# GDN decays without a DRAM round trip, another address for the weight buffers, one modulation sum per chunk in the first MLP, and SSD decay rows issued one step later

## The chip, the cores and the metric

The program runs on one core of a Trainium2 chip, alone. The metric is the time of one execution on the device in microseconds (us). The kernel before was run three times: 2693.74, 2696.27 and 2699.25 us.

## The reference

The input is 512 tokens of width 1024 (`x`), and eight stages follow each other, all in float32: a gated-delta-rule mixer (GDN), a convolutional feed-forward (ffn0), a chunked attention, a second feed-forward (ffn1), an S5 state-space mixer, an MLP (mlp0), an SSD mixer, an MLP (mlp1), and a final norm. The pieces that the change touches:

```python
# GDN, per head and chunk of 64 tokens
gcum  = cumsum(g)                                  # g: log decay per token
decay = where(causal, exp(gcum[:, None] - gcum[None, :]), 0)
m     = where(strict, (k*beta) @ k.T * decay, 0)   # then (m + I)^-1 applied to v*beta, k*beta*exp(gcum)
attn  = (q @ k.T) * decay
q_dec = q * exp(gcum)
...
# second block: modulation from a condition vector c
mod = silu(c) @ ada_w[i] + ada_b[i]                # 1024 x 6144 per layer
sh1, sc1, g1, sh2, sc2, g2 = split(mod, 6)
h = rmsnorm(x) * (1 + sc) + sh
mlp: a = relu(h @ w1); y = (a*a) @ w2
...
# SSD, per head and chunk of 128 tokens
l_mat  = exp(segsum(dt*a))                         # decays inside a chunk
y_diag = (C B^T * l_mat) @ xdt
y_off  = (C @ state_before) * exp(cumsum(dt*a))
```

## The kernel before, in words

**Layout.** Activations lie with the feature on the partition and the 512 tokens along the row: eight tiles `h` of 128x512. To keep float32 accuracy TensorE (PE) gets every operand as a sum of two reduced floats, `hi` and `lo`. So one chunk of weights (128x1024, 512 KB, one column block of 128 outputs) costs a DMA into `raw` (L296), a cast to `hi` on ScalarE (ACT, L306), a subtraction to `lo` on VectorE (DVE, L307), and 24 matmuls of 128x128 by 128x512 in `mm_ch`: for each of 8 row blocks `hi` by `xh` (L348), `hi` by `xl` (L349), `lo` by `xh` (L350). `raw`, `hi` and `lo` have three buffers each; `next()` keeps the split one chunk ahead and the loads three. The moving operand is named by the stage: `xh`/`xl` for a stage's normed input, `ah`/`al` for the inner activations of feed-forward and MLP, `goh`, `aoh`, `soh` for the outputs of GDN, attention and S5 or SSD.

**Where tiles lie.** Tiles get their addresses in the order in which the program makes them. `xh` and `xl` come before `rb` and `rcol` (L248), and all weight buffers and the pools of the stages come behind them. Each 128-wide block of weights and each moving tile row begins at a multiple of 512 bytes from its buffer's start, so the distance between a weight block and a moving tile, taken modulo 512 bytes, is fixed per pair of buffers.

**Order.** Instructions run in order on each engine's queue, and so do the DMA issues on SyncE's (SP). A scheduler at build time sets the order in each queue from the order in the code and the buffers that come free.

**GDN.** `gdn_gates` makes the cumulated log decays of all heads, writes them as rows to DRAM (`grow`), and then, for each of 8 heads, loads them back to all partitions (`gd`), subtracts the column's value and adds a mask (on GpSimd, POOL, L683 and L684, or, for the first four heads, on DVE, L687), takes the exponential on ACT (L689) and writes the 128x512 result to DRAM (`gD`). `gdn_core` of a head loads `gD` back as `D`, loads `exp` rows as `eg`, multiplies `q` into `eg` on POOL (L840), makes `ke` (ACT, L821), the products `s<-kq` (PE, L834), `N` and `AT` (DVE, L836 and L838), and inverts: 15 small steps `td`, `Xd` on DVE (L850, L852) on the diagonal blocks, which come back through DRAM (`Nd<-gN`), a mask product `Nm` on POOL (L873), and block steps on PE. `gdn_proj` makes q, k and v of a head: projection, convolution, Silu (L778).

**Background work.** `next()` calls `step_bg(self.bgrate)`: that many steps of a queue of generators per chunk of weights. `ada_bg(q)` makes a third of the modulation vector: 32 steps, each a 512 KB load (`araw<-ada`, two buffers) and one multiply-add into `acc` (DVE, L1145), then 16 small matmuls `bg<-par,acc` (L1150) that sum it. `shift_bg` makes a product of the modulation shift with weight columns: multiply-adds into `sacc` (L1402), and a matmul `bg<-ones,sacc` (L1393) per chunk. In ffn1 the rate is 1 or 2, and its last value, 2, stays on in mlp0, where the queue holds `shift_bg` for SSD, `ada_bg(2)` and `shift_bg` for mlp1.

**SSD.** Four groups of 8 heads. The decays' rows lie in DRAM (`srow`). Per group two `D` tiles (128x2048, four heads each) and four `E` tiles are loaded from it, the `E` with two rows spread over 64 partitions each. `ssd_exps` subtracts on DVE, and step 1 of `ssd_core` takes the exponential.

Of the kernel before, what the change touches and what calls it, by code (L numbers as in the profile page):

```python
# [224 lines left out]
class Net:  # L225
    def __init__(self, ctx, tc, aps, pcols, out):
# [21 lines left out]
        rc = self.cpool.tile([P, 8], F32, name="rcol")  # L248
# [384 lines left out]
    def gdn_gates(self, gg, g1, wk):  # L633
# [31 lines left out]
        ga = gg.tile([P, 3, 32], F32, name="gga")  # L665
# [12 lines left out]
        self.gD = self.dram.tile([8, P, T], F32, name="gD")  # L678
        for hd in range(8):
            d = wk.tile([P, 4, P], F32, tag="Nm", name=self.nm("gd"))  # L680
            nc.sync.dma_start(out=d, in_=self.grow[0, 4 * hd:4 * hd + 4, :].partition_broadcast(P))
            if hd > 3:
                gp.tensor_tensor(out=d, in0=d, in1=bc(ga[:, 0, 4 * hd:4 * hd + 4], P), op=ALU.subtract)  # L683
                gp.tensor_tensor(out=d, in0=d, in1=self.p("nincl").unsqueeze(1).to_broadcast([P, 4, P]), op=ALU.add)  # L684
            else:
                for c in range(4):
                    v.scalar_tensor_tensor(out=d[:, c, :], in0=d[:, c, :], scalar=ga[:, 0, 4 * hd + c:4 * hd + c + 1],  # L687
                                           in1=self.p("nincl"), op0=ALU.subtract, op1=ALU.add)
            s.activation(d, d, AF.Exp)  # L689
            nc.sync.dma_start(out=self.gD[hd], in_=d.rearrange("p c t -> p (c t)"))  # L690

    def gdn(self):
# [3 lines left out]
        with es:  # L696
# [4 lines left out]
            self.eye16 = g1.tile([32, 256], F32, name="geye")  # L701
# [16 lines left out]
            nc.sync.dma_start(out=self.eye16, in_=self.aps["eye16"])  # L718
# [6 lines left out]
            for name, i in self.gdn_seq():  # L725
# [41 lines left out]
    def gdn_proj(self, wk, hd):  # L767
        s = self.nc.scalar
        taps = [self.p(f"a_conv{j}") for j in range(4)]
        kq = wk.tile([P, 2, T], F32, tag="kq", name=self.nm("kq"))  # L770
# [8 lines left out]
        return kq, vv  # L779

    def gdn_core(self, wk, hd, kq, vv):
# [19 lines left out]
        Dt, eg = tl("D"), tl("eg")  # L801
        nc.sync.dma_start(out=Dt.rearrange("p c t -> p (c t)"), in_=self.gD[hd])
# [1269 lines left out]
```

## Time and profile before

| what | value |
|---|---|
| median of three runs | 2696.27 us |
| the profiled execution: its own time | 2695.84 us |
| the profiled execution: its span in the trace | 2694.0 us |
| PE busy, DVE busy, ACT busy, POOL busy | 2614.5, 1943.8, 1182.6, 114.8 us |
| granted PE clock, mean over the span | 0.989 |

The span is what the trace covers from the first to the last instruction; 1.84 us of the execution's time lie around it. The stages stand in the span, roughly: GDN to 380 us, ffn0 to 760, attention to 1020, ffn1 to 1380, S5 to 1580, mlp0 to 1960, SSD to 2325, mlp1 to the end. A granted clock of 1.00 is PE's higher level, 2.4 GHz, and 0.5 the lower, 1.2 GHz. The time printed for one matmul is its latency; how fast a row of them goes is read from the distance of their starts.

### The profile page before, as it was taken

The page shows a single profiled execution, that of the slowest core. Times are in us where ns is not written, and L with a number is a line of the kernel's source. Part 1 is how long each engine was busy: PE and PEld are TensorE (multiplying, and loading weights), DVE is VectorE, ACT ScalarE, POOL GpSimd, SP SyncE. Part 2 cuts the span into 40 slices and gives each one's busy share as a digit, 9 for nine tenths or more (in the row PEclk, how much of TensorE's full clock was granted, in tenths as well). Part 3 has the DMA queues.
Part 4 walks back from the last instruction along what each step waited for, and adds up shares of the span by engine and source line. Part 5 has one row for each costly group of instructions (what it writes and reads, how often), then busy time and mean ns, then how long its engine had stood idle before and what let it go on. Part 6 is the DMA issues. An engine that isn't in the chain of part 4 may idle for free. (4 is left out here: it accounts for less than half of the span.)

```text
span 2694.0 us, 36720 instructions
## 1 busy us (share of the span) xinstructions
PE 2614.5 (97%) x13978; PEld 2108.1 (78%) x13978; DVE 1943.8 (72%) x3614; ACT 1182.6 (44%) x1868; POOL 114.8 (4%) x150
## 2 busy tenths in 40 slices
PE   8899999999999999999998999899998999999998
PEld 6777777888877877888877788788877877788886
DVE  7887889997656588979888577644588778844443
ACT  7555554343445465423264352233464434533332
POOL 0211100000002110000002000000000000000000
PEclk9999999999999999999999999899999999999999
DMA  5433223544334337766639348433233432232322
GB/s 163 139 84 86 68 87 91 170 150 143 107 115 111 99 89 234 237 200 219 215 100 298 118 136 277 160 99 94 86 118 110 141 104 98 85 102 94 99 97 71
DMA packets 172705, 356.33 MB, mean 132 GB/s; under 512 B 44048, under 2 KB 81648, under 8 KB 171504
## 3 DMA queue, kind: packets, MB, share of 16 engines
q1 hardware_dynamic: 163056, 349.78, 41.2%
q10 hardware_dynamic: 9472, 4.20, 0.5%
q8 instruction: 110, 1.80, 0.3%
q14 instruction: 67, 0.55, 0.1%
HBM read 324.00 MB, written 25.72 MB: 130 GB/s over the span
## 5 line engine op out<-in xcount | busy, mean ns | idle before, releaser
L306 ACT CAST hi<-raw 128x1024 fp32r<-128x1024 f32 (+1 forms) x416 | 433.0, 1042 | 868.7 <-PE mm L349 718.8
L348 PE MATMUL mm<-xh,hi 128*128 128x512 f32 x1824 | 734.4, 403 | 17.9 <-ACT hi L306 9.2
L350 PE MATMUL mm<-xh,lo 128*128 128x512 f32 x1824 | 723.7, 398 | 2.1 <-DVE lo L307 2.0
L349 PE MATMUL mm<-xl,hi 128*128 128x512 f32 x1824 | 722.0, 396 | 0.0
L307 DVE TENSOR_TENSOR lo<-raw,hi 128x1024 fp32r<-128x1024 f32 (+1 forms) x416 | 503.5, 1211 | 214.0 <-ACT hi L306 208.9
L348 PEld LDWEIGHTS mm<-xh,hi 128*128 128x128 f32 x1824 | 346.6, 190 | 95.7 <-ACT hi L306 11.2
L350 PEld LDWEIGHTS mm<-xh,lo 128*128 128x128 f32 x1824 | 345.9, 190 | 81.3 <-DVE lo L307 3.9
L349 PEld LDWEIGHTS mm<-xl,hi 128*128 128x128 f32 x1824 | 346.5, 190 | 73.8 <-issue 2.3
L348 PE MATMUL mm<-ah,hi 128*128 128x512 f32 x864 | 337.5, 391 | 0.0
L349 PE MATMUL mm<-al,hi 128*128 128x512 f32 x864 | 336.4, 389 | 0.0
L350 PE MATMUL mm<-ah,lo 128*128 128x512 f32 x864 | 336.3, 389 | 0.0
L581 DVE SCALAR_TENSOR_TENSOR h<-mm,mods,h 128x512 f32<-128x512 f32 x96 | 71.8, 749 | 177.1 <-PE mm L350 176.8
L348 PEld LDWEIGHTS mm<-ah,hi 128*128 128x128 f32 x864 | 162.2, 188 | 34.5 <-ACT hi L306 1.2
L609 DVE SCALAR_TENSOR_TENSOR cv<-cvr,par,cv 128x511 f32<-128x511 f32 (+2 forms) x248 | 187.0, 754 | 2.7 <-ACT cv L607 0.8
L350 PEld LDWEIGHTS mm<-ah,lo 128*128 128x128 f32 x864 | 162.2, 188 | 34.0 <-DVE lo L307 0.3
L349 PEld LDWEIGHTS mm<-al,hi 128*128 128x128 f32 x864 | 162.2, 188 | 33.6
L1145 DVE SCALAR_TENSOR_TENSOR acc<-araw,condt,acc 128x1024 f32<-128x1024 f32 x93 | 119.1, 1280 | 34.6 <-DMA araw<-ada 34.0
L579 DVE TENSOR_TENSOR h<-mm,h 128x512 f32<-128x512 f32 x112 | 76.6, 686 | 51.5 <-PE mm L350 51.1
L350 PE MATMUL mm<-soh,lo 128*128 128x512 f32 x256 | 100.5, 393 | 0.5 <-DVE lo L307 0.5
L348 PE MATMUL mm<-soh,hi 128*128 128x512 f32 x256 | 100.8, 400 | 0.1
L349 PE MATMUL mm<-sol,hi 128*128 128x512 f32 x256 | 100.7, 394 | 0.0
L600 DVE TENSOR_TENSOR cvr<-mm,rb 128x512 f32<-128x512 f32 x112 | 76.6, 684 | 32.6 <-PE mm L350 25.1
(526 smaller groups left out, 3602.0 us busy)
## 6 DMA issues: line engine op xcount, KB each, us to landing
raw<-mlp SPq DMA_DIRECT2D x128, 512.0 KB, 3.5
araw<-ada SPq DMA_DIRECT2D x96, 512.0 KB, 4.4
raw<-f_up SPq DMA_DIRECT2D x88, 512.0 KB, 3.8
raw<-m_in SPq DMA_DIRECT2D x40, 512.0 KB, 4.5
raw<-a_in SPq DMA_DIRECT2D x32, 512.0 KB, 4.3
raw<-f_down SPq DMA_DIRECT2D x32, 512.0 KB, 4.5
raw<-b_kv SPq DMA_DIRECT2D x16, 512.0 KB, 3.6
raw<-s_glu SPq DMA_DIRECT2D x16, 512.0 KB, 4.2
```

The source lines that it names most:

```text
L306: self.nc.scalar.copy(hi[:, :sz], raw[:, :sz])
L307: self.nc.vector.tensor_tensor(out=lo[:, :sz], in0=raw[:, :sz], in1=hi[:, :sz].bitcast(F32), op=ALU.subtract)
L348: self.nc.tensor.matmul(ps, a, xh, start=(start and k == 0), stop=False)
L349: self.nc.tensor.matmul(ps, a, xl, start=False, stop=False)
L350: self.nc.tensor.matmul(ps, b, xh, start=False, stop=(stop and k == n - 1))
L579: nc.vector.tensor_tensor(out=self.h[ot], in0=ps, in1=self.h[ot], op=ALU.add)
L581: nc.vector.scalar_tensor_tensor(out=self.h[ot], in0=ps, scalar=g[:, ot:ot + 1], in1=self.h[ot], op0=ALU.mult, op1=ALU.add)
L600: nc.vector.tensor_tensor(out=pr, in0=ps, in1=r, op=ALU.mult)
L609: nc.vector.scalar_tensor_tensor(out=t[:, d:], in0=ps[:, :T - d], scalar=taps[n - 1 - d], in1=t[:, d:], op0=ALU.mult, op1=ALU.add)
L1145: v.scalar_tensor_tensor(out=acc, in0=raw, scalar=cond[:, k:k + 1], in1=acc, op0=ALU.mult, op1=ALU.add)
```

## The change

- **GDN.** The loop over heads leaves `gdn_gates`. A new `gdn_decay`, called at the start of a head's `gdn_proj`, loads `D` and `eg` of that head from `grow` and makes `D` in its place: two 128x512 operations on DVE and the exponential on ACT. `gD` and its 16 transfers are gone. `eg` and `Nm` go from POOL to DVE. `Xd` is loaded from DRAM by a DMA per head instead of being copied from `geye`.
- **Addresses.** `rcol` grows from 8 to 24 floats, so all that is made behind it lies 64 bytes further; `geye` goes and `gga` is padded.
- **PSUM banks.** Before the last output projection of GDN, and in the last quarter of attention's, `set_lanes()` opens all five `mm` banks instead of two.
- **Background.** `ada_bg` waits one step more before its matmuls; `shift_bg` issues its matmul one step later, with three `sacc` buffers; `mlp` sets `bgrate = 1`.
- **SSD.** The code issues the fourth `E` tile and both `D` tiles of the next group one step later; the second half's subtraction moves into the next group's step 0.

The core of the diff:

```diff
-        rc = self.cpool.tile([P, 8], F32, name="rcol")
+        rc = self.cpool.tile([P, 24], F32, name="rcol")
...
-        self.gD = self.dram.tile([8, P, T], F32, name="gD")
-        for hd in range(8):
-            d = wk.tile([P, 4, P], F32, tag="Nm", name=self.nm("gd"))
-            nc.sync.dma_start(out=d, in_=self.grow[0, 4 * hd:4 * hd + 4, :].partition_broadcast(P))
-            if hd > 3:
-                gp.tensor_tensor(out=d, in0=d, in1=bc(ga[:, 0, 4 * hd:4 * hd + 4], P), op=ALU.subtract)
-                gp.tensor_tensor(out=d, in0=d, in1=self.p("nincl").unsqueeze(1).to_broadcast([P, 4, P]), op=ALU.add)
-            else:
-                for c in range(4):
-                    v.scalar_tensor_tensor(out=d[:, c, :], in0=d[:, c, :], scalar=ga[:, 0, 4 * hd + c:4 * hd + c + 1],
-                                           in1=self.p("nincl"), op0=ALU.subtract, op1=ALU.add)
-            s.activation(d, d, AF.Exp)
-            nc.sync.dma_start(out=self.gD[hd], in_=d.rearrange("p c t -> p (c t)"))
+
+    def gdn_decay(self, wk, hd):
...
+        rows = slice(4 * hd, 4 * hd + 4)
+        d, eg = [wk.tile([P, 4, P], F32, tag=t, name=self.nm(t), bufs=2) for t in ("D", "eg")]
+        for x, out in enumerate((d, eg)):
+            nc.sync.dma_start(out=out, in_=self.grow[x, rows, :].partition_broadcast(P))
+        nc.vector.tensor_tensor(out=d, in0=d, in1=bc(self.ga[:, 0, rows], P), op=ALU.subtract)
+        nc.vector.tensor_tensor(out=d, in0=d, in1=self.p("nincl").unsqueeze(1).to_broadcast([P, 4, P]), op=ALU.add)
+        nc.scalar.activation(d, d, AF.Exp)
+        return d, eg
...
+                    if i == 2:
+                        self.set_lanes()
                     self.proj_out("a_out", [outs.pop(2 * i), outs.pop(2 * i + 1)], 512, 2, last=(i == 3))
...
-        Dt, eg = tl("D"), tl("eg")
-        nc.sync.dma_start(out=Dt.rearrange("p c t -> p (c t)"), in_=self.gD[hd])
-        nc.sync.dma_start(out=eg, in_=self.grow[1, 4 * hd:4 * hd + 4, :].partition_broadcast(P))
...
-        gp.tensor_tensor(out=eg, in0=r3(q, 4), in1=eg, op=ALU.mult)
+        v.tensor_tensor(out=eg, in0=r3(q, 4), in1=eg, op=ALU.mult)
...
-        v.tensor_copy(Xd.rearrange("p j i -> p (j i)"), self.eye16)
+        nc.sync.dma_start(out=Xd.rearrange("p j i -> p (j i)"), in_=self.aps["eye16"])
...
-        gp.tensor_tensor(out=m, in0=N, in1=self.lv.unsqueeze(1).to_broadcast([P, 4, P]), op=ALU.mult)
+        v.tensor_tensor(out=m, in0=N, in1=self.lv.unsqueeze(1).to_broadcast([P, 4, P]), op=ALU.mult)
...
             yield
         yield
+        yield
         ps = self.bank("bg")
...
-            if i > 1:
+            if i > 2:
                 ps = self.bank("bg")
-                nc.tensor.matmul(ps[:, 0:1], accs[i - 2], self.ones[:, 0:1], start=True, stop=True)
-                v.tensor_copy(out[:, i - 2:i - 1], ps[:, 0:1])
+                nc.tensor.matmul(ps[:, 0:1], accs[i - 3], self.ones[:, 0:1], start=True, stop=True)
+                v.tensor_copy(out[:, i - 3:i - 2], ps[:, 0:1])
...
             acts = {}
+            self.bgrate = 1
...
+            if g:
+                self.ssd_exps(g, 1)
...
-            for j in range(4):
-                E = self.stile("E")
-                nc.sync.dma_start(out=E, in_=AP(self.srow.tensor, self.srow.offset + (32 + 8 * g + 2 * j) * T,
-                                                [[T, 2], [0, 64], [1, T]]))
-                S["E"].append(E)
+            for j in range(3):
+                self.ssd_erow(g, j)
...
+            if j == 1:
+                self.ssd_erow(g, 3)
+            if j == 2 and g < 3:
+                self.ssd_rows(g + 1, 0)
...
-            if j % 2 == 1 and g < 3:
-                self.ssd_rows(g + 1, j // 2)
...
-            self.ssd_exps(g + 1, 1)
+            self.ssd_rows(g + 1, 1)
```

What this does to the order on the engines stands here for three places. The first is ACT's queue in GDN, at the second head's `ke` (L821 before, L818 after; `junk` are the row sums of squares that precede it, `gd` the exponentials of the decays). Before:

```order
85 L814 ACTIVATE junk_1000,ss_978<-s_146_979 128x128
86 L689 ACT_TABLE_LOAD
87 L689 ACTIVATE gd_326<-gd_326 128x512
88 L689 ACTIVATE gd_332<-gd_332 128x512
89 L814 ACTIVATE junk_1002,ss_978<-s_148_981 128x128
90 L821 ACTIVATE ke_1011<-s_146_979,gge 128x128
```

The same place in the changed kernel:

```order
84 L811 ACTIVATE junk_949,ss_925<-s_140_928 128x128
85 L811 ACTIVATE junk_951,ss_925<-s_140_928 128x128
86 L811 ACTIVATE junk_953,ss_925<-s_140_928 128x128
87 L811 ACTIVATE junk_955,ss_925<-s_140_928 128x128
88 L818 ACTIVATE ke_958<-s_138_926,gge 128x128 x4
```

The exponentials of other heads' decays no longer stand between the row sums and `ke`. They stand further up and further down the queue, one table load each: three heads' before this place, the fourth during the first head's inversion.

The second is DVE's queue in the middle of mlp0, at the last multiply-adds of `ada_bg(2)`. `lo` is the split of a weight chunk, `ra` and `al` the activations of an up-projection chunk, and `mods` takes up what the `bg<-par,acc` matmuls on PE have summed. Before:

```order
2604 L307 TENSOR_TENSOR lo_16123<-raw_16038,hi_16122 128x1024
2605 L1145 SCALAR_TENSOR_TENSOR acc_15471<-araw_16043,condt,acc_15471 128x1024
2606 L1612 TENSOR_TENSOR ra_16071<-mm_16046,ra_16071 128x512
2607 L1145 SCALAR_TENSOR_TENSOR acc_15471<-araw_16084,condt,acc_15471 128x1024
2608 L568 TENSOR_TENSOR al_16075<-ra_16071,ah_16074 128x512
2609 L307 TENSOR_TENSOR lo_16176<-raw_16082,hi_16175 128x1024
2610 L1145 SCALAR_TENSOR_TENSOR acc_15471<-araw_16087,condt,acc_15471 128x1024
2611 L1612 TENSOR_TENSOR ra_16115<-mm_16090,ra_16115 128x512
2612 L1153 TENSOR_TENSOR mods<-bg_16128,par 128x32
```

The changed kernel, at the last multiply-add:

```order
2624 L1144 SCALAR_TENSOR_TENSOR acc_15582<-araw_16682,condt,acc_15582 128x1024
2625 L307 TENSOR_TENSOR lo_16069<-raw_15990,hi_16068 128x1024
2626 L1613 TENSOR_TENSOR ra_16020<-mm_15995,ra_16020 128x512
2627 L1144 SCALAR_TENSOR_TENSOR acc_15582<-araw_16723,condt,acc_15582 128x1024
2628 L568 TENSOR_TENSOR al_16024<-ra_16020,ah_16023 128x512
2629 L1144 SCALAR_TENSOR_TENSOR acc_15582<-araw_16764,condt,acc_15582 128x1024
2630 L307 TENSOR_TENSOR lo_16110<-raw_16031,hi_16109 128x1024
2631 L1613 TENSOR_TENSOR ra_16061<-mm_16036,ra_16061 128x512
```

The multiply-adds keep their pace of two per weight chunk; the scheduler has drawn them up as before. `mods` followed one row behind the last of them, and now comes 55 rows and 21 weight chunks (`lo`) later, and with it the matmuls on PE: they stood in the middle of the chunk that PE had just begun, and now stand 20 chunks behind the one that the last multiply-add was drawn up with.

The third is SP's queue in SSD, at the transfers of the first group's last and the second group's first `E`. Before:

```order
685 L296 DMA raw_18377<-m_in 128x1024
686 L1784 DMA D_18368<-srow 128x2048
687 L1873 DMA E_18216<-srow 128x1x512
688 L1873 DMA E_18824<-srow 128x1x512
689 L296 DMA raw_18437<-m_in 128x1024
690 L1873 DMA E_18826<-srow 128x1x512
691 L1784 DMA D_18490<-srow 128x2048
692 L296 DMA raw_18515<-m_in 128x1024
```

The changed kernel:

```order
676 L296 DMA raw_18340<-m_in 128x1024
677 L1785 DMA D_18374<-srow 128x2048
678 L1790 DMA E_18312<-srow 128x1x512
679 L1790 DMA E_18789<-srow 128x1x512
680 L296 DMA raw_18402<-m_in 128x1024
681 L1790 DMA E_18791<-srow 128x1x512
682 L1785 DMA D_18512<-srow 128x2048
683 L296 DMA raw_18478<-m_in 128x1024
```

Nothing moved: the transfers of `D`, `E` and the weights follow each other as before, here and in all four groups.

## Rows read from the trace of the kernel before

**Rows 1.** The page: busy us by engine.
```profile
PE 2614.5 (97%) x13978; PEld 2108.1 (78%) x13978; DVE 1943.8 (72%) x3614; ACT 1182.6 (44%) x1868; POOL 114.8 (4%) x150
```

**Rows 2.** GDN by windows; PEclk is the granted clock, then DMA share, GB/s.
```profile
core 0: us, PE busy (x) PEld busy (x) DVE busy (x) ACT busy (x) POOL busy (x), PEclk, DMA share, GB/s
80.00:100.00 20.00, 13.13 (x44) 9.96 (x43) 18.87 (x56) 10.55 (x23) 10.95 (x8) 0.77 0.36 124
...
100.00:360.00 260.00, 253.31 (x2253) 203.73 (x2251) 207.92 (x688) 132.47 (x385) 29.56 (x45) 1.00 0.28 81
```

**Rows 3.** Waits of PE in 60 to 340 us: total, times, longest.
```profile
PE s L834 <- ACT ke L821: 5.4, 2, 4.3
PE s L834 <- DVE brk L827: 2.6, 1, 2.6
```

**Rows 4.** GDN's timeline on ACT: start, us, what, [idle before <-what ended it].
```profile
83.23 0.63 ACT L689 ACTIVATE gd<-gd 128x512 f32<-128x512 f32 x1 [1.74 <-POOL gd L684]
```

**Rows 5.** The timeline on PE at the L1150 matmuls: ffn1's, then mlp0's.
```profile
1355.78 1.84 PE L1150 MATMUL bg<-par,acc 128*128 128x4 f32 x16
...
1702.10 0.40 PE L350 MATMUL mm<-xh,lo 128*128 128x512 f32 x1
1710.02 3.57 PE L1150 MATMUL bg<-par,acc 128*128 128x4 f32 x16 [7.52 <-DVE acc L1145]
...
1719.09 0.40 PE L349 MATMUL mm<-xl,hi 128*128 128x512 f32 x1
```

**Rows 6.** SSD's timeline on ACT and PE at its one stall.
```profile
2037.28 1.05 ACT L306 CAST hi<-raw 128x1024 fp32r<-128x1024 f32 x1 [7.76 <-DMA raw<-m_in]
...
2042.77 0.47 PE L348 MATMUL mm<-xh,hi 128*128 128x512 f32 x1 [3.96 <-DVE cv L609]
```

**Rows 7.** SSD by windows, columns as in rows 2.
```profile
2040.00:2060.00 20.00, 14.45 (x52) 11.59 (x53) 17.43 (x52) 12.15 (x13) 0.00 (x0) 0.74 0.24 80
```

**Rows 8.** Waits of PE at 340 to 390, 980 to 1030, 1365 to 1380 us.
```profile
PE mm L348 <- DVE h L579: 1.3, 5, 0.3
...
PE mm L348 <- DVE h L579: 1.1, 4, 0.4
...
PE bg L1393 <- DVE sacc L1402: 1.0, 1, 1.0
```

**Rows 9.** mlp1's timeline on PE: a stretch of `xh` matmuls, one of `ah`.
```profile
2428.49 0.40 PE L348 MATMUL mm<-xh,hi 128*128 128x512 f32 x1
...
2472.46 0.40 PE L348 MATMUL mm<-ah,hi 128*128 128x512 f32 x1
...
2515.80 0.39 PE L350 MATMUL mm<-ah,lo 128*128 128x512 f32 x1
```

**Rows 10.** GDN's lines on DVE and ACT: xcount | busy us, mean ns | idle before.
```profile
L852 DVE TENSOR_TENSOR Xd<-Xd,td 32x15 f32<-32x15 f32 (+7 forms) x120 | 28.9, 240 | 1.9
...
L850 DVE TENSOR_TENSOR td<-Nd,Xd 32x15 f32<-32x15 f32 (+7 forms) x120 | 26.0, 217 | 3.0 <-DMA Nd<-gN 1.2
...
L687 DVE SCALAR_TENSOR_TENSOR gd<-gd,gga,par 128x128 f32<-128x128 f32 x16 | 4.5, 348 | 1.0 <-DMA gd<-grow 1.0
...
L847 DVE COPY Xd<-geye 32x256 f32<-32x256 f32 x8 | 2.1, 277 | 1.4 <-DMA gX<-Xd 1.4
...
L778 ACT ACT_TABLE_LOAD x6 | 7.7, 1283 | 3.6 <-DVE cv L609 3.6
```

**Rows 11.** One line each: count, ns min/median/max; GDN's `Xd` and SSD's `y`.
```profile
L852 DVE TENSOR_TENSOR Xd<-Xd,td x120: 152/198/1286, 80.9 to 332.4; 32x15 f32<-32x15 f32 x16, 32x28 f32<-32x28 f32 x16, 32x39 f32<-32x39 f32 x16, 32x48 f32<-32x48 f32 x16
...
L1892 DVE TENSOR_TENSOR y<-y,z x16: 679/688/695, 2021.2 to 2292.6; 128x512 f32<-128x512 f32 x16
```

**Rows 12.** GDN's timeline on DVE at the first head: last `N`, then `td`.
```profile
72.21 0.60 DVE L836 SCALAR_TENSOR_TENSOR N<-s,brk,D 128x128 f32<-128x128 f32 x2
...
80.37 0.48 DVE L850 TENSOR_TENSOR td<-Nd,Xd 32x15 f32<-32x15 f32 x1 [1.23 <-DMA Nd<-gN]
```

**Rows 13.** SSD, 2008 to 2054 us: GB/s in 40 slices.
```profile
GB/s 48 75 185 283 66 50 50 50 50 50 100 335 399 143 52 50 100 290 146 52 64 121 267 333 383 303 53 50 50 59 50 50 52 48 50 96 272 169 32 0
```

More of the change, by code (lines that the diff above doesn't have):

```diff
@@ L663, in gdn_gates @@
         nc.tensor.matmul(ps[:, 32:64], self.ones, g, start=True, stop=True)
-        ga = gg.tile([P, 3, 32], F32, name="gga")
+        self.ga = ga = gg.tile([P, 112], F32, name="gga")[:, :96].rearrange("p (x n) -> p x n", x=3)
         v.tensor_copy(ga[:, 0, :], ps[:, 0:32])
@@ L677, in gdn_gates @@
         nc.sync.dma_start(out=self.grow.rearrange("x r c -> r x c"), in_=rows)
-        self.gD = self.dram.tile([8, P, T], F32, name="gD")
-        for hd in range(8):
-            d = wk.tile([P, 4, P], F32, tag="Nm", name=self.nm("gd"))
-            nc.sync.dma_start(out=d, in_=self.grow[0, 4 * hd:4 * hd + 4, :].partition_broadcast(P))
-            if hd > 3:
-                gp.tensor_tensor(out=d, in0=d, in1=bc(ga[:, 0, 4 * hd:4 * hd + 4], P), op=ALU.subtract)
-                gp.tensor_tensor(out=d, in0=d, in1=self.p("nincl").unsqueeze(1).to_broadcast([P, 4, P]), op=ALU.add)
-            else:
-                for c in range(4):
-                    v.scalar_tensor_tensor(out=d[:, c, :], in0=d[:, c, :], scalar=ga[:, 0, 4 * hd + c:4 * hd + c + 1],
-                                           in1=self.p("nincl"), op0=ALU.subtract, op1=ALU.add)
-            s.activation(d, d, AF.Exp)
-            nc.sync.dma_start(out=self.gD[hd], in_=d.rearrange("p c t -> p (c t)"))
+    def gdn_decay(self, wk, hd):
+        nc = self.nc
+        rows = slice(4 * hd, 4 * hd + 4)
[6 more added lines that the diff above has]
+        return d, eg
     def gdn(self):
@@ L700, in gdn @@
             self.gXl = [g1.tile([64, 4, 64], F32, name=f"gXl{i}") for i in range(2)]
-            self.eye16 = g1.tile([32, 256], F32, name="geye")
             wk = es.enter_context(self.tc.tile_pool(name="gdn", bufs=2))
@@ L717, in gdn @@
             nc.sync.dma_start(out=self.lv, in_=self.aps["lv"])
-            nc.sync.dma_start(out=self.eye16, in_=self.aps["eye16"])
             for x in self.gXT + self.gXl:
@@ L769, in gdn_proj @@
         taps = [self.p(f"a_conv{j}") for j in range(4)]
+        dec = self.gdn_decay(wk, hd)
         kq = wk.tile([P, 2, T], F32, tag="kq", name=self.nm("kq"))
@@ L778, in gdn_proj, with gdn_core @@
             s.activation(dst, cv, AF.Silu)
-        return kq, vv
-    def gdn_core(self, wk, hd, kq, vv):
+        return (kq, vv) + dec
+    def gdn_core(self, wk, hd, kq, vv, Dt, eg):
         nc = self.nc
@@ L1034, in attn @@
                 else:
+                    if i == 6:
+                        self.set_lanes()
                     w = self.next("b_out", 512)
@@ L1384, in shift_bg @@
         raws, accs = [], []
-        for i in range(len(chunks) + 2):
+        for i in range(len(chunks) + 3):
             if i < len(chunks):
@@ L1390, in shift_bg @@
                     nc.sync.dma_start(out=raws[i][hf], in_=self.aps[name][c, :, hf * T:(hf + 1) * T])
-            if i > 1:
+            if i > 2:
                 ps = self.bank("bg")
-                nc.tensor.matmul(ps[:, 0:1], accs[i - 2], self.ones[:, 0:1], start=True, stop=True)
-                v.tensor_copy(out[:, i - 2:i - 1], ps[:, 0:1])
+                nc.tensor.matmul(ps[:, 0:1], accs[i - 3], self.ones[:, 0:1], start=True, stop=True)
+                v.tensor_copy(out[:, i - 3:i - 2], ps[:, 0:1])
             if 0 < i <= len(chunks):
-                accs.append(self.apool.tile([P, P], F32, tag="sacc", name=self.nm("sacc"), bufs=2))
+                accs.append(self.apool.tile([P, P], F32, tag="sacc", name=self.nm("sacc"), bufs=3))
                 for k in range(KT):
@@ L1784, in ssd_rows, with ssd_erow @@
         self.nc.sync.dma_start(out=d, in_=self.srow[0, h0:h0 + 4, :].partition_broadcast(P))
+    def ssd_erow(self, g, j):
+        E = self.stile("E")
+        self.nc.sync.dma_start(out=E, in_=AP(self.srow.tensor, self.srow.offset + (32 + 8 * g + 2 * j) * T,
+                                             [[T, 2], [0, 64], [1, T]]))
+        self.S[g]["E"].append(E)
     def ssd_exps(self, g, hf):
```

## The prediction

> **What bounds the kernel now.** I read the busy times first. PE is busy 2614.5 of 2694.0 us [rows 1]. So a gain can come from two places: the roughly 80 us in which PE stands, with the lower clock that follows, and the rate at which its matmuls go on from one another. The windows of 20 us then show where PE stands. Three places stick out, each a wait behind which the granted clock drops from 2.4 to 1.2 GHz for a while: GDN at 80 to 100 us [rows 2 to 4], mlp0 at 1702 us [rows 5], SSD at 2037 to 2054 us [rows 6, 7]. The rest is small change: 6.7 us in which PE stands in the other 260 us of GDN [rows 2], and an us here and there at the output projections and shift sums [rows 8].
>
> **mlp0's modulation sum.** PE works in order, and behind the matmul that starts at 1702.10 it has the 16 of `bg<-par,acc`, which wait 7.52 us for the last multiply-add of `ada_bg(2)` and then take 3.57 us where the same 16 took 1.84 in ffn1; the 13 matmuls after them run slower too, and only the one at 1719.09 is at full pace [rows 5]. Due in that stretch, from 1702.33 to 1719.09 (16.76 us), are 1.84 + 13 x 0.229 = 4.82 us. So 11.9 us are lost. In the changed order `bg<-par,acc` comes 20 chunks of weights behind the place of the last multiply-add, and a chunk is 24 x 0.229 = 5.5 us of PE: the sum is ready some 100 us before PE asks. DVE still does two multiply-adds per chunk and still waits for `araw`, but the splits `lo` are as far ahead of PE as before, when PE did not wait for one. **-11.9 us.** What speaks against it is that DVE, in order behind `araw`, may deliver a `lo` late; that is a rival below. The shift sums' extra step takes away the wait for `sacc` in ffn1 [rows 8]: **-1.0 us**.
>
> **The address of the weight buffers.** Between two stretches of mlp1 in which PE never waits, the pace differs by the moving tile: 192 matmuls on `xh` and `xl` start between 2428.49 and 2472.46, so 43.97 / 192 = 229.0 ns apart; the 192 on `ah` and `al` that follow start between 2472.46 and 2515.80, so 43.34 / 191 = 226.9 ns [rows 9]. Both read the same weight buffers, and both are 128x512. What differs is where they lie: in the built program's addresses a moving `ah` tile begins at the same place modulo 512 bytes as a weight block, an `xh` tile 64 bytes past it. The change shifts the weight buffers by 64 bytes (16 floats of `rcol`) and `ah`, which is made later, along with them, but not `xh`. Then both distances are zero. There are 1824 x 3 = 5472 matmuls on `xh`, times 2.1 ns: 11.5 us. The 768 of GDN's projections (32 chunks of 24) stand in a stage where PE waits for others now and then, so I count half of their 1.6 us: **-10.7 us**. The bounds are 0 (the place is not the cause) and, if the absolute place counts, a loss (both below).
>
> A page speaks against this term. The Trainium skill, "SBUF — State Buffer", section "Who interferes with whom", gives PE two independent read ports, one for moving data and one for weights, and says that only the port pair shared by VectorE and GpSimd causes contention. By that rule no distance between the two could matter, and the sum would lose these 10.7 us. The rows' 2.1 ns show some cause that goes with the tile, without saying which, so the rule makes a rival and not the forecast.
>
> **GDN.** In 80 to 100 us PE is busy 13.13 us, so 6.9 us are lost, and the clock of 0.77 costs another 0.23 x 20 = 4.6 us [rows 2]. The longer wait, 4.3 us, is for `ke` on ACT [rows 3], and ACT in turn had stood in order at exponentials of `gd` that POOL had not delivered [rows 4]. That is the order that the change removes: no `gd` stands ahead of the second head's `ke` any more. What it adds, by kind:
> - DVE gets per head two operations for `D`, one for `eg` and one for `Nm`, all 128x512. The nearest row, SSD's `y`, is 0.688 us [rows 11]: 32 x 0.688 = 22.0 us. It loses the 16 of L687 (4.5) and the copies of `Xd` (2.1) [rows 10]. The `td` and `Xd` steps have means of 217 and 240 ns [rows 10] about a median of 198, with single ones up to 1286 [rows 11]; if it is POOL's operations that stretch these, 120 x (19 + 42) ns = 7.3 us go. Net 22.0 - 4.5 - 2.1 - 7.3 = +8.1 us.
> - ACT keeps eight exponentials, but spread out they cost table loads: by the order six more in all, 6 x 1.283 = 7.7 us [rows 10].
> - Of the DMAs, 24 of 256 KB (into `gd`, into `gD`, out of it) become 8, and 8 small ones for `Xd` join them, all issued on SP. The DMA share there is 0.28 [rows 2], so I count them at nothing.
>
> In 100 to 360 us DVE is busy 207.92 of 260 us and ACT 132.47 [rows 2]; +8.1 and +7.7 over eight heads is about 1 us each per head of 32 us, and PE's own work hides that, unless it falls into a chain that PE waits for. One place is visible. In the first head `N` ends at 72.81 and `td` begins at 80.37, when `Nd` has come back through DRAM [rows 12]: 7.6 us. In the new order DVE has seven operations between them, some 5.4 us by their like, so it stands about 2.2 us at `td`; the last steps of v's convolution are queued behind it, and v's Silu (ACT) and PE's transposes behind those. I count 2.3 us of waiting there, as much again at the following `s<-kq`, and some 2 us of lower clock, so 6.5 of the 11.5 us stay. The bounds: all 11.5 us gone, or all the added DVE and ACT time on the path (the slow rival). I take the difference, since the new waits rest on the trace's own latency of `Nd`: **-5 us**.
>
> **PSUM banks.** The last projections use two banks, and PE waits for `h` (L579) to empty them, 1.3 us in GDN and 1.1 in attention [rows 8]. Five banks let PE run ahead: **-2.0 us** (0 to -2.4).
>
> **SSD.** The stall is a chain of transfers. ACT waits 7.76 us for a weight chunk, and PE 3.96 us for what follows [rows 6]; in 2040 to 2060 us 5.55 us of PE's time and 0.26 x 20 = 5.2 us of clock are lost, 10.7 together [rows 7]. Meanwhile the DMA engines move 50 GB/s for long stretches, in which the `E` tiles are under way, and 300 to 400 when weights flow [rows 13]. In the code the edit moves these transfers, but SP's queue comes out the same, operation by operation, and so does PE's at this place. What does move is DVE's second-half subtraction, which is not what ACT waits for. **0 us** (-10.7 if the stall goes, +4 if a second wait like PE's 3.96 us arises where that subtraction now stands).
>
> **Sum.** -11.9 - 1.0 - 10.7 - 5 - 2 + 0 = -30.6 us on the profiled execution's 2695.84 us, which lies 0.43 us under the median of 2696.27: 2665 us.
>
> **The rivals.**
> 1. The place of the buffers gives nothing: the 2.1 ns have another cause that stays with `xh`. For it: no row shows how two reads of PE would meet. Against: weights, shape and clock are the same, and only the place is left that I can name. 2665 + 10.7 = 2676 us.
> 2. The absolute place of the moving tile counts. Then `xh` does not gain, and `ah`, moved to `xh`'s old place modulo 512, loses 2.1 ns on 864 x 3 = 2592 matmuls, 5.4 us: 2681 us. No row separates this from the forecast, since all weight buffers lie alike.
> 3. The SSD stall goes as well, because weights and `E` meet differently in time: 2665 - 10.7 = 2654 us.
> 4. mlp0's stall changes its place: DVE, held at `araw`, hands over a `lo` late, and PE waits there instead: 2665 + 11.9 = 2677 us. Against: the same pace before, without such a wait.
> 5. Slower: DVE becomes GDN's bound. If the 22.0 us of added operations and the 7.7 us of table loads all lie in the chain from one head's `N` to the next head's `ke`, and nothing is freed for them, GDN costs 29.7 us more and gains nothing: 2665 + 5 + 29.7 = 2700 us. It decides itself where PE's waits grow to over 3 us per head, for eight heads. Against: DVE has 52 us free in 260.
>
> **How the numbers follow.** A measurement tells about 0.2% (5.4 us) from no change. Forecast (2658 to 2672) 0.50; rival 1 0.17; rival 2 0.07; rival 3 0.09; rival 4 0.06; rival 5 in full 0.05, and in part (2680 to 2695) 0.06. Only rival 5 reaches no change or the slower side: same 0.05, slower 0.04, and the rest of it still faster, so faster 0.91. The range must hold 0.8: the forecast and rivals 1, 2 and 4 make that up, so it goes from 2655 to 2684.
>
> **What would show it.** In the changed kernel's trace: the pace of `xh` matmuls in mlp1 at 227 ns and that of `ah` unchanged (rival 1: 229 and 227; rival 2: 229 and 229). No wait of PE at `bg<-par,acc`, and a clock of 1.00 from 1600 to 1740 us. In 80 to 100 us PE busy over 15 us, nothing of `gd`, `eg`, `Nm` on POOL, and `td`, `Xd` at a mean of 200 ns. In SSD the 50 GB/s stretches and a stall of about 10 us as before. The prediction is wrong above all if the pace of `xh` stays, or if PE waits for DVE in every head of GDN.

## The result

The changed kernel takes 2666.91 us (median of four runs, 2665.68 to 2670.15) where the kernel before takes 2695.84 in the same comparison: a ratio of 0.9893, with a 95% interval of 0.9876 to 0.9911. That is 28.9 us less; forecast were 30.6 less, 2665 us. The sum came out, but several of its terms did not, and their errors cancelled.

The page of the changed kernel, its span and busy times, beside [rows 1]:

```profile
span 2664.3 us, 36647 instructions
...
PE 2598.1 (98%) x13978; PEld 2108.1 (79%) x13978; DVE 1936.5 (73%) x3622; ACT 1188.3 (45%) x1874; POOL 86.9 (3%) x126
```

PE does the same 13978 matmuls in 16.4 us less of busy time. Its standing time, span minus busy, falls from 79.5 to 66.2 us.

The windows of the changed kernel at the places of [rows 2, 5, 7]; the columns are those of rows 2. The two last are SSD's stall, which lies 27 us earlier:

```profile
80.00:100.00 20.00, 19.51 (x186) 14.13 (x185) 17.66 (x55) 10.62 (x30) 2.88 (x4) 1.00 0.48 141
...
340.00:360.00 20.00, 17.66 (x82) 13.60 (x81) 12.91 (x34) 7.00 (x19) 0.00 (x0) 0.91 0.17 54
360.00:380.00 20.00, 15.55 (x54) 11.68 (x53) 16.50 (x32) 13.68 (x20) 1.14 (x6) 0.83 0.25 79
...
1700.00:1720.00 20.00, 20.00 (x90) 16.57 (x89) 11.49 (x15) 7.81 (x10) 0.00 (x0) 1.00 0.41 132
2000.00:2020.00 20.00, 15.04 (x85) 12.07 (x84) 13.78 (x34) 5.35 (x8) 0.00 (x0) 0.91 0.42 140
2020.00:2040.00 20.00, 18.67 (x74) 14.98 (x75) 17.14 (x48) 14.65 (x15) 0.00 (x0) 0.84 0.33 99
```

The early stall in GDN is gone (PE 19.51 of 20 us, where it had 13.13), and so is mlp0's. SSD's stall stands as it stood. New is a stall at 340 to 380 us, at the end of GDN, with a clock of 0.91 and 0.83. The kernel before had, in the same windows:

```profile
340.00:360.00 20.00, 20.00 (x184) 15.75 (x183) 13.01 (x40) 9.11 (x26) 1.15 (x4) 1.00 0.17 55
360.00:380.00 20.00, 18.41 (x74) 12.70 (x73) 18.66 (x34) 14.46 (x21) 0.00 (x0) 1.00 0.09 26
```

The pace of mlp1's matmuls, as in [rows 9], again one stretch on `xh` and the next on `ah`:

```profile
2399.99 0.39 PE L348 MATMUL mm<-xh,hi 128*128 128x512 f32 x1
...
2443.51 0.39 PE L348 MATMUL mm<-ah,hi 128*128 128x512 f32 x1
...
2486.80 0.39 PE L350 MATMUL mm<-ah,lo 128*128 128x512 f32 x1
```

192 matmuls on `xh` in 43.52 us are 226.7 ns each, and `ah` takes 43.29 / 191 = 226.7. Before it was 229.0 and 226.9.

Where the time went can be read from the L348 matmuls, of which there are 3184 in each trace: the table has the start of the one that has n of them before it, in both traces, and the difference:

| n, place | before, us | after, us | ahead by |
|---|---|---|---|
| 64, early GDN | 80.81 | 82.25 | -1.4 |
| 192, late GDN | 279.52 | 261.00 | 18.5 |
| 320, ffn0 begun | 415.39 | 409.74 | 5.6 |
| 832, attention begun | 790.99 | 782.33 | 8.7 |
| 1536, S5 begun | 1415.89 | 1402.20 | 13.7 |
| 1856, mlp0, before the sum | 1676.93 | 1664.30 | 12.6 |
| 1920, mlp0, behind the sum's old place | 1735.76 | 1707.82 | 27.9 |
| 2112, mlp0, behind its new place | 1867.13 | 1841.11 | 26.0 |
| 2688, mlp1 begun | 2341.02 | 2312.79 | 28.2 |
| last | 2679.36 | 2649.55 | 29.8 |

So GDN is 18.5 us ahead at n = 192 and 5.6 at n = 320. The first of these flatters the change: the order of PE's work is another one too, and before that matmul the changed kernel has done 140 of the heads' small matmuls (`s`) fewer, 950 against 1090. The time that PE stands is free of this. Up to 340 us it stands 15.5 us, where it stood 25.4, and from 340 to 400 us 6.8, where it stood 1.6. The lower clock has only moved: 10.2 us of it lie between 84 and 101 us before, and as many between 354 and 375 us now. So GDN wins some 10 us of standing and gives 5 of them back at its end. The giving back was in no term of the forecast.

### The profile page after: what moved, and what is told of

Read it like the earlier page. It is cut to its first block, busy times and chain, and to the rows that moved or that the text cites. A ratio compares the mean times of both kernels' runs of the same rounds, so it can differ in the third digit from the quotient of the medians.

```text
span 2664.3 us, 36647 instructions
## 1 busy us (share of the span) xinstructions
PE 2598.1 (98%) x13978; PEld 2108.1 (79%) x13978; DVE 1936.5 (73%) x3622; ACT 1188.3 (45%) x1874; POOL 86.9 (3%) x126
## 5 line engine op out<-in xcount | busy, mean ns | idle before, releaser
L348 PE MATMUL mm<-xh,hi 128*128 128x512 f32 x1824 | 726.4, 398 | 21.6 <-ACT hi L306 10.0
L348 PEld LDWEIGHTS mm<-xh,hi 128*128 128x128 f32 x1824 | 344.8, 189 | 98.1 <-ACT hi L306 12.5
L348 PE MATMUL mm<-ah,hi 128*128 128x512 f32 x864 | 338.0, 391 | 0.0
L348 PEld LDWEIGHTS mm<-ah,hi 128*128 128x128 f32 x864 | 162.3, 188 | 34.3 <-ACT hi L306 0.8
L348 PE MATMUL mm<-soh,hi 128*128 128x512 f32 x256 | 100.9, 401 | 3.2 <-ACT soh L567 3.2
```

Source lines behind the costliest of these rows:

```text
L348: self.nc.tensor.matmul(ps, a, xh, start=(start and k == 0), stop=False)
```

## The experiments

**Does the place of the weight buffers set the pace?** Three kernels are the kernel before with nothing but tiles moved (in the cuts of code, a remark behind # names the run).

```diff
-        rc = self.cpool.tile([P, 8], F32, name="rcol")
+        rc = self.cpool.tile([P, 24], F32, name="rcol")     # e1_place
...
-            t = self.cpool.tile([P, 1], F32, name=f"eps{int(round(-math.log10(v)))}")
+            t = self.cpool.tile([P, 9], F32, name=f"eps{int(round(-math.log10(v)))}")[:, :1]     # e2_all64
...
+        rc = self.cpool.tile([P, 88], F32, name="rcol")     # e3_far
```

> The kernel before with rcol at 24 floats instead of 8 and nothing else: weight buffers and all pools lie 64 bytes further, xh and xl stay. Theory A (the distance between a moving tile and a weight block, modulo 512 bytes, sets the pace): xh matmuls in mlp1 at 226.9 ns instead of 229.0, ah unchanged at 226.9, time 10 to 11.5 us below before, about 2685 us. Theory B (the absolute place of the moving tile): xh stays at 229.0, ah goes to 229.0, time 5 us above before. Theory C (the place is nothing): both paces and the time as before; the 11 us of the result then came from elsewhere.

> The kernel before with two early small tiles wider, so that everything behind them, xh and xl too, lies 64 bytes further: all absolute places change as in e1, all distances stay as before. Theory A: xh 229.0, ah 226.9, time as before (2696 us, within 5). Theory B: the paces of e1 (xh and ah change against before), time 5 to 11 us away. Theory C: as before.

> The kernel before with rcol at 88 floats: xh and xl now lie 256 bytes (modulo 512) from the weight blocks, ah still at 0. Theory A: xh matmuls get slower than before, to about 231 ns, the pace that the attention's aoh tiles, which lie at 256, have in the trace of before; 5472 x 2 ns is 11 us above before, about 2707 us. Theories B and C: no such loss in xh alone; C says 2696.

The same stretch of mlp1 as above, first `xh` and first `ah` matmul, in the trace of e1_place:

```profile
2422.47 0.39 PE L348 MATMUL mm<-xh,hi 128*128 128x512 f32 x1
...
2465.99 0.39 PE L348 MATMUL mm<-ah,hi 128*128 128x512 f32 x1
```

In that of e2_all64:

```profile
2429.82 0.40 PE L348 MATMUL mm<-xh,hi 128*128 128x512 f32 x1
...
2473.78 0.40 PE L348 MATMUL mm<-ah,hi 128*128 128x512 f32 x1
```

And in that of e3_far:

```profile
2421.78 0.39 PE L348 MATMUL mm<-xh,hi 128*128 128x512 f32 x1
...
2465.30 0.39 PE L348 MATMUL mm<-ah,hi 128*128 128x512 f32 x1
```

That is 43.52, 43.96 and 43.52 us for 192 matmuls: 226.7, 229.0 and 226.7 ns, while `ah` stays within 226.7 to 226.9 in all of them. e2 moves everything by the same 64 bytes and changes nothing (2697.15 us, one run), so it is not the absolute place: theory B falls, and C with e1. But e3 falls out of theory A as it was put: at a distance of 256 bytes `xh` is as fast as at 0, where 231 ns were expected (2687.81 us, one run).

The time of e1 is 2690.11 us against 2695.65, a ratio of 0.9981 (0.9972 to 0.9991): 5.5 us less, where 10 to 11.5 were expected. By the differences of the matmuls' starts, as in the table above, e1 wins 9.6 us behind GDN and loses 2.3 before it: the early stall is still there in this kernel (its PE is busy 12.95 us in 80 to 100 us). Whether the stall eats the pace's gain or the place is worth only 5.5, the reverse in the changed kernel was to tell:

```diff
-        rc = self.cpool.tile([P, 24], F32, name="rcol")
+        rc = self.cpool.tile([P, 8], F32, name="rcol")      # the changed kernel, e12_undo_place
```

> The changed kernel with rcol back at 8 floats and nothing else, so the weight buffers and pools lie where they lay before and xh is 64 bytes (modulo 512) off the weight blocks again. Theory (in e1 the pace gained 9.6 us outside GDN, and GDN lost 2.3 of it by a stall that fell otherwise): without that stall the place is worth its full price in the changed kernel, so this one is 9 to 11 us slower than the changed kernel, about 2677 us, with xh at 228.9 ns. Rival: e1's 5.5 us is the place's price, then about 2672 us.

It takes 2675.06 us, a ratio of 0.9931 (0.9917 to 0.9944) to the kernel before. Against the changed kernel that is 8.2 us by the medians and 0.0038 x 2695 = 10.2 us by the two ratios, with `xh` back at 229.0 ns. Between the two traced executions it is 7.6 us, and 7.3 between before and e1. So the place is worth some 5 to 10 us; that the stall ate a part of it in e1 is not shown.

**Which distances are slow?** One kernel more with all of `xh` at another distance, and one with every `xh` and `xl` tile at a distance of its own:

```diff
+        rc = self.cpool.tile([P, 120], F32, name="rcol")    # e9_mod128
...
-        self.xh = [self.cpool.tile([P, T], F32R, name=f"xh{k}") for k in range(KT)]
-        self.xl = [self.cpool.tile([P, T], F32R, name=f"xl{k}") for k in range(KT)]
+        self.xh = [self.cpool.tile([P, T + 8], F32R, name=f"xh{k}")[:, :T] for k in range(KT)]     # e5_scan
+        self.xl = [self.cpool.tile([P, T + (8 if k < 6 else 0)], F32R, name=f"xl{k}")[:, :T] for k in range(KT)]
```

> The kernel before with rcol at 120 floats: xh and xl now lie 128 bytes (modulo 512) from the weight blocks, ah still at 0. e1 (0) and e3 (256) are fast, before (64) slow. Theory A128 (places that agree modulo 128 are fast): xh in mlp1 at 226.9 ns. Theory A256 (they must agree modulo 256): 229 ns or more, and a time of before or above.

> The kernel before with the sixteen xh and xl tiles 32 bytes apart in their place modulo 512: their distances to a weight block are 128, 160 ... 352 (xh of row blocks 0 to 7), 384, 416, 448, 480, 0, 32, 64, 64 (xl of row blocks 0 to 7). Theory A as first put (any distance but 0 costs): only the xl of row block 4 is at 226.9 ns, the others at 229 to 233. Theory A narrowed after e1 to e3 (a band of distances around 64 costs, 0 and 256 do not): the xl of row blocks 6 and 7, at 64, keep a step of 229 or more, and most others go to 226.9. Theory C: all alike.

e9_mod128, same stretch:

```profile
2441.17 0.40 PE L348 MATMUL mm<-xh,hi 128*128 128x512 f32 x1
...
2485.96 0.39 PE L348 MATMUL mm<-ah,hi 128*128 128x512 f32 x1
```

44.79 us, 233.3 ns, and 2710.73 us for the kernel (one run). So the price by distance, with all `xh` and `xl` alike, is: 0 none, 64 some 2 ns, 128 some 6 ns, 256 none. That fits a period of 256 bytes and no shorter one. Attention's `aoh` does not fit it: it lies at 256 before and in e3, and the steps from one matmul on `aoh` or `aol` to the next, where PE neither waits nor has the lower clock, have means of 229 to 232 ns there, in rows far shorter than mlp1's. The scan does not fit it: it is slow throughout (2709.2 us, one run), and the steps behind the `xh` tile at 256 and the `xl` tile at 0, which by the rule should be fast, have medians of 234 and 229 ns. In the scan consecutive moving tiles of one chunk also differ in their place from each other, which they do in no other kernel here. So both the distance to the weights and something between the moving tiles may count. What the mechanism is stays open.

**mlp0.** The kernel before with the rate alone, without the added steps:

```diff
+            self.bgrate = 1
             heads, self.heads = self.heads, None
```

> The kernel before with bgrate = 1 in the MLPs and nothing else; the modulation sum and the shift sums keep their old steps. Theory: the rate alone moves the sum's matmuls on PE far enough behind the last multiply-add, so the wait of 7.5 us and the lower clock behind it go: 12 us below before, about 2684 us. Rival: it is the extra step before the matmuls that moves them, then PE still waits here, and the time is within 4 us of before.

2684.01 us against 2695.65, a ratio of 0.9961 (0.9947 to 0.9975): 11.6 us less. In its trace the sum's matmuls come late and unhindered, like ffn1's in [rows 5]:

```profile
1808.29 1.84 PE L1150 MATMUL bg<-par,acc 128*128 128x4 f32 x16
```

In the changed kernel they start at 1805.74, and DVE's last multiply-add there starts at 1698.03:

```profile
1695.60 1.28 DVE L1144 SCALAR_TENSOR_TENSOR acc<-araw,condt,acc 128x1024 f32<-128x1024 f32 x1 [0.40 <-DMA araw<-ada]
...
1698.03 1.28 DVE L1144 SCALAR_TENSOR_TENSOR acc<-araw,condt,acc 128x1024 f32<-128x1024 f32 x1 [0.53 <-DMA araw<-ada]
```

DVE still waits for `araw`, and PE has no wait at all from 1600 to 1900 us, in either kernel. The rate is the cause; the added steps are not needed for it.

**GDN alone, and its end.** e6 is the kernel before with the hunks of GDN but not `set_lanes()`; e7 is the changed kernel without the first `set_lanes()`:

```diff
                 else:
-                    if i == 2:
-                        self.set_lanes()
                     self.proj_out("a_out", [outs.pop(2 * i), outs.pop(2 * i + 1)], 512, 2, last=(i == 3))
```

> The kernel before with GDN's part alone (decays made in place per head, eg and Nm on DVE, Xd loaded by DMA), without the change of banks, addresses of the weight buffers, background and SSD. Theory: GDN gains more than the 5 us forecast, since the stall at 80 to 100 us goes whole: 9 to 11 us below before, about 2686 us, with PE's wait for ke gone and td, Xd at a mean of 193 ns. Rival: what GDN gains here is lost again at its own end, where DVE is full, and the time is within 5 us of before.

> The changed kernel without set_lanes() before GDN's last projection (attention's stays). Theory: with five banks PE runs ahead of DVE, which is full with h, xl and the squares, and then stands 4.0 us in one piece at the start of ffn0 and goes to its lower clock; with two banks it waits in pieces of 0.2 to 0.3 us and keeps the clock. Then the time is 3 to 4 us below the changed kernel's, about 2663 us, and the clock at 340 to 380 us is 1.00 instead of 0.87. Rival: DVE sets this end either way, and the time is the changed kernel's, 2667 us.

e6 takes 2687.32 us against 2696.13, a ratio of 0.9968 (0.9957 to 0.9979): 8.8 us less, where 9 to 11 were expected. In the difference of the starts it is 17.6 us ahead at n = 192, with the same 950 `s` before it as the changed kernel, and 6.8 at n = 320, in ffn0. Some 2 us more come in mlp0 (6.4 at n = 1856, 8.5 at n = 1920), where its trace has 10.2 us of lower clock against 13.7; e8_ssd, which changes nothing there either, has 10.2 too. So GDN itself is worth about 7 us. Two of its windows:

```profile
100.00:340.00 240.00, 238.18 (x2074) 193.41 (x2073) 196.32 (x668) 139.66 (x376) 16.74 (x28) 1.00 0.28 82
340.00:360.00 20.00, 15.60 (x77) 11.83 (x76) 10.29 (x30) 7.37 (x20) 0.00 (x0) 0.85 0.08 27
```

PE is nearly never idle from 100 to 340 us, and then stands, with DVE (10.29) and ACT (7.37) half idle as well. That reads as the serial end of the last heads' recurrence, for which no other work is left; no run shows it apart. Against before, PE stands 9.0 us less up to 340 us (16.4 against 25.4) and 3.5 us more from 340 to 400 us (5.1 against 1.6).

e7 takes 2666.86 us, as the changed kernel (ratio 0.9893, 0.9878 to 0.9907). By the time the theory of the banks falls and the rival holds, though an interval of 8 us could hide the 2 us below. PE's waits at GDN's end, in the timeline of the changed kernel:

```profile
352.05 1.10 PE L952 MATMUL s<-par,o 128*128 128x128 f32 x4 [1.56 <-DVE o L948]
...
368.97 0.80 PE L348 MATMUL mm<-xh,hi 128*128 128x512 f32 x1 [3.99 <-DVE h L579]
```

And in e7_nobank:

```profile
352.32 1.10 PE L950 MATMUL s<-par,o 128*128 128x128 f32 x4 [3.62 <-DVE o L946]
...
366.36 0.49 PE L348 MATMUL mm<-goh,hi 128*128 128x512 f32 x1 [0.19 <-DVE h L579]
...
368.32 0.47 PE L348 MATMUL mm<-xh,hi 128*128 128x512 f32 x1 [0.30 <-DVE h L579]
```

With five banks the long wait stands at the start of ffn0, with two it stands before the last output rows `o`; ffn0 gets going at 368 to 369 us in both. So the end is set by the chain through `o` and then DVE's work on `h`, and the banks choose where PE stands. The clock of the theory is in the trace all the same: in 360 to 380 us e7 has

```profile
360.00:380.00 20.00, 19.38 (x80) 14.61 (x80) 18.65 (x34) 15.10 (x21) 1.15 (x6) 0.99 0.23 78
```

against 0.83, and with 288 of the L348 matmuls done it is 2.3 us ahead of the changed kernel (385.66 against 387.99). With 1856 done nothing is left of that (1664.28 and 1664.30): e7 has 3.4 us more of lower clock at 428.6 us, behind a wait of 2.46 us for `lo`, and the changed kernel, behind one of 2.41 us, has none. Attention's banks no run takes away. There PE's waits for `h` add up to 0.5 us in the changed kernel and to 1.1 before.

**DVE or POOL for `eg` and `Nm`.** The changed kernel with these two back on POOL:

```diff
-        v.tensor_tensor(out=eg, in0=r3(q, 4), in1=eg, op=ALU.mult)
+        gp.tensor_tensor(out=eg, in0=r3(q, 4), in1=eg, op=ALU.mult)
...
-        v.tensor_tensor(out=m, in0=N, in1=self.lv.unsqueeze(1).to_broadcast([P, 4, P]), op=ALU.mult)
+        gp.tensor_tensor(out=m, in0=N, in1=self.lv.unsqueeze(1).to_broadcast([P, 4, P]), op=ALU.mult)
```

> The changed kernel with eg and Nm back on POOL (11 us less on DVE, all else as changed). Theory: POOL's operations stretch DVE's small steps, so the mean of td and Xd rises again from 193 ns towards 217 and 240, and since GDN's end sets what the stage gains, the time stays within 4 us of the changed kernel's 2667. Rival: DVE's 22 us of added operations were costly, and without 11 of them the kernel is 5 us or more faster.

2676.23 us, a ratio of 0.993 (0.9913 to 0.9947): 9 to 10 us slower than the changed kernel, although DVE has 11 us less to do. Both guesses miss. DVE's small steps in the changed kernel, as in [rows 10]:

```profile
L849 DVE TENSOR_TENSOR Xd<-Xd,td 32x15 f32<-32x15 f32 (+7 forms) x120 | 23.2, 194 | 2.1
...
L847 DVE TENSOR_TENSOR td<-Nd,Xd 32x15 f32<-32x15 f32 (+7 forms) x120 | 23.0, 192 | 2.0
```

And in e10_pool, with the two operations on POOL:

```profile
L849 DVE TENSOR_TENSOR Xd<-Xd,td 32x15 f32<-32x15 f32 (+7 forms) x120 | 24.9, 207 | 2.1
...
L847 DVE TENSOR_TENSOR td<-Nd,Xd 32x15 f32<-32x15 f32 (+7 forms) x120 | 23.0, 192 | 2.6 <-DMA Nd<-gN 0.8
...
L837 POOL TENSOR_TENSOR eg<-kq,eg 128x512 f32<-128x512 f32 x8 | 12.7, 1592 | 136.1 <-DMA eg<-grow 117.7 <-ACT kq L778 18.5
...
L870 POOL TENSOR_TENSOR Nm<-N,glv 128x512 f32<-128x512 f32 x8 | 10.3, 1288 | 97.9 <-DVE N L833 80.4 <-DVE ro L428 17.6
```

The stretch of `td` and `Xd` comes back by 1.7 us only, so most of the 8.7 us that it was worth in [rows 10] came from the `gd` operations on POOL. The trace of before says the same: against the medians of the same steps in the changed kernel, the seven steps that overlap a `gd` operation, all between 80 and 95 us, are 6.0 us too long together, and those that overlap an `eg` or `Nm` 2.0.

What costs the 9 us is not shown. PE is busy 233.23 us in 100 to 340 us instead of 237.99. An operation takes 1.3 to 1.6 us on POOL and 0.68 on DVE (`eg`'s and `Nm`'s means in the changed kernel are 684 and 682 ns), so its latency is one candidate. But no wait of PE ends on POOL; PE's longest new one, 2.6 us before an `s<-kq`, ends on DVE. And the scheduler has drawn up another order: at n = 128 PE has done 574 of the `s`, where the changed kernel has done 476. No run tells the two apart.

**SSD.**

> The kernel before with SSD's part alone. Theory: the transfers keep their order, so the stall of about 10.7 us at 2037 to 2054 us stays, and the time is before's, 2696 us within 3. Rival: the later subtraction moves the stall, by 5 us or more either way.

SSD's part alone, in the kernel before, gives 2694.12 us (one run), with PE's wait of 3.3 us and ACT's of 7.1 in place. The edit does nothing that can be measured. What does, in the changed kernel:

```diff
-        self.nc.sync.dma_start(out=E, in_=AP(self.srow.tensor, self.srow.offset + (32 + 8 * g + 2 * j) * T,
-                                             [[T, 2], [0, 64], [1, T]]))
+        for i in range(2):
+            self.nc.sync.dma_start(out=E[64 * i:64 * i + 64, :],
+                                   in_=AP(self.srow.tensor, self.srow.offset + (32 + 8 * g + 2 * j + i) * T,
+                                          [[0, 64], [1, T]]))
```

> The changed kernel with each E tile loaded by two transfers of 64 partitions from one row each, instead of one transfer whose outermost dimension counts two rows. Theory: the stall in SSD comes from E moving at 50 GB/s on few of the DMA engines with a weight chunk queued behind; spread out, E takes about 1 to 2 us, the wait of ACT for the weights goes, and the time falls by 7 to 11 us to about 2658 us. Rival: the stall is set by when the E and D buffers come free; then PE still loses about 10 us at that place and the time stays within 4 us of 2667.

The busy share of the 16 DMA engines, in tenths, and their rates, in 1980 to 2026 us by 40 slices, in the changed kernel, beside [rows 13], and ACT's wait there:

```profile
DMA  1111493111116971128711267998111111112788
GB/s 48 50 50 50 110 333 98 48 50 48 50 52 210 427 306 45 50 71 203 265 46 50 64 148 287 390 354 232 50 50 50 53 57 46 50 48 75 271 223 303
```

```profile
2010.55 1.05 ACT L306 CAST hi<-raw 128x1024 fp32r<-128x1024 f32 x1 [7.15 <-DMA raw<-m_in]
```

In e11_halves:

```profile
DMA  9899950000000000998479101879995000017874
GB/s 413 235 292 233 287 185 21 0 0 14 0 0 0 0 0 0 399 392 310 128 210 360 25 0 21 221 192 392 438 383 150 29 12 0 0 28 246 235 232 178
```

The long stretches at 50 are gone, and with them ACT's 7.15 us wait for a weight chunk; the weights of this stretch land 4.9 us behind their issue in the median, where it was 9.1. e11 takes 2662.07 us, a ratio of 0.988 (0.9865 to 0.9894), 4.8 us under the changed kernel by the medians; by the matmuls' starts SSD gains 5.0 us. The intervals of the two ratios overlap, so the time alone does not settle it; the stretch in the trace does. It is the best of the kernels here, though less than the 7 to 11 us expected, for a smaller wait takes the old one's place:

```profile
2020.34 0.79 PE L350 MATMUL mm<-xh,lo 128*128 128x512 f32 x1 [1.49 <-DVE lo L307]
```

PE waits there for DVE's `lo`, and the clock is 0.84 in 2020 to 2040 us, as it was in the changed kernel. The Trainium skill, "DMA: Bandwidth & Descriptors", section "Why a DMA increments its semaphore by 16 and not by 1", says that a transfer is split over the largest number of engines up to 16 that divides the slowest dimension on both sides; with a leading dimension of two that is two engines. The trace agrees as far as it goes: where the rate is 50 GB/s, the 16 engines are busy at between one and two tenths, as two of 16 would be, and with the halves at up to nine tenths. `D` and the weights move in those slices too, so the rate of a half by itself is not shown.

## Why the prediction was right, and where not

- **mlp0's sum**: forecast -11.9 us, measured -11.6 (e4). The step holds as worked out, including the margin of some 100 us (1698 to 1806).
- **The address**: forecast -10.7, measured -5.5 (e1) and -8 to -10 (e12), and 226.7 ns in place of 229.0 in the traces of e1 and after. The term holds in kind and was somewhat too large. The Trainium skill, "SBUF — State Buffer", section "Who interferes with whom", by whose rule no distance between the moving data and the weights could matter, is not borne out: e1 and e2 move the same buffers by the same 64 bytes, and only e1, where the distance changes, gains. What failed is the generalisation under the term: "the same place modulo 512" is too narrow, since for `xh` 256 is as fast, and 128 is worse than the 64 that it started from.
- **GDN**: forecast -5, measured -8.8 in e6, of which about 7 are GDN's own. The sum was close by two errors, and that is luck. The step that failed first is the waiting at `Nd`: the forecast took from the old trace that `Nd` comes 7.6 us behind `N`, and so counted 2.2 us at `td`, 2.3 us on PE twice, and 2 us of clock. The first head in the changed kernel, on DVE:

```profile
65.72 0.60 DVE L833 SCALAR_TENSOR_TENSOR N<-s,brk,D 128x128 f32<-128x128 f32 x2
...
71.74 0.17 DVE L847 TENSOR_TENSOR td<-Nd,Xd 32x15 f32<-32x15 f32 x1
```

  `td` begins 5.4 us behind the end of `N`, straight after the operations that now stand between, and waits for nothing. PE loses 0.81 us at v's transposes and 0.36 at `s<-kq`, at the full clock, so nearly all of the early stall goes. The DMAs, which the forecast counted at nothing, are the likely reason. The window of 60 to 80 us, before and after:

```profile
60.00:80.00 20.00, 20.00 (x142) 18.67 (x141) 15.54 (x30) 15.74 (x27) 4.69 (x4) 1.00 0.77 247
```

```profile
60.00:80.00 20.00, 19.19 (x137) 17.82 (x136) 18.29 (x49) 12.81 (x23) 0.00 (x0) 1.00 0.34 104
```

  The DMA share beside `Nd`'s trip falls from 0.77 to 0.34; no run shows this effect by itself. The second error was not counted at all: the standing at the end of the stage, 3.5 us more in e6 and 5.2 in the changed kernel. The ledger of DVE was right in size (22.1 us added by the trace's rows for `D`, `eg`, `Nm`; 8.7 us of stretch gone where 7.3 were counted), ACT's table loads come out six more as counted (16 against 10), and neither bounds the stage: from 60 to 345 us PE's waits come to 3.2 us, where they were 13.4. The cause given for the stretch was right in kind; `gd` had most of it, `eg` and `Nm` little (e10).
- **The clock** in GDN's and SSD's stalls was counted too high: 4.6 and 5.2 us, shares of a whole window in which PE partly stood. At the lower level PE was busy 7.8 us at 84 to 101 us and 7.5 us at 2043 to 2054 us, and a 128x512 matmul at that level starts every 0.43 us (changed kernel, 370 to 374 us) instead of every 0.23; so some 3.5 us were lost at each place.
- **The banks**: forecast -2.0, of which GDN's part measures 0 (e7); attention's part was not run by itself, and its waits for `h` fall by 0.6 us. The step took PE's waits for `h` as lost time that more banks give back. In GDN they were the way in which DVE's pace showed; freed there, PE waits in one piece behind.
- **The shift sums**: forecast -1.0; a wait of 0.8 us stands at the same place in the changed kernel, where 1.0 stood before.
- **SSD**: forecast 0, measured 0 (e8). Reading the order of the transfers, instead of the code, gave it.
- **The rivals**: that the place gives nothing fell (e1, e12), the absolute place fell (e2), a DVE bound in GDN fell (e6, e10), and mlp0's stall did not move, nor did SSD's go.

The measured parts, -11.6 (e4), -8.8 (e6) and -5.5 to -10 (e1, e12), make 26 to 30, and the whole is 28.9. That the parts add up fits this, but each of them is known to 3 to 5 us only. That the forecast of 30.6 lies so near is in part luck: some 3 us too much for the address and as much for banks and shift sums stand against 4 us too little for GDN.

## What to carry to other kernels

Price a stage by what PE can reach at its end, not only by the waits inside it: GDN, which ends with little work for any engine, gave back a third to a half of what it had won, and more banks there only moved the wait. A latency read from the old trace holds only while the traffic beside it stays the same. Before a difference of two starts is called a gain, count the work that lies before each. When an edit moves transfers in the code, read the built order first; and when a transfer crawls, look at its outermost dimension. Where a matmul stream never waits and still runs at two paces, compare where its operands lie.

## What was not expected of the hardware

The distance between the moving tiles `xh`, `xl` and the weight blocks, modulo 512 bytes, changes the pace of their 128x512 matmuls: 226.7 ns at 0 and at 256, 229.0 at 64, 233.3 at 128, all in mlp1 with nothing waiting and the granted clock at 1.00. The kernel with 128 took 2710.73 us and that with 256 took 2687.81, one run each; the two differ in the length of `rcol` alone. The kernel with sixteen different places at once is slow at nearly all of them, and `aoh`, in its short rows, is slower than `xh` at the same 256, so no rule here is complete.
